# Thirteen of sixteen expert pairs through DRAM with a late read-back, and four smaller moves, in a fused two-block transformer kernel

## The chip, the cores and the metric

The kernel runs as one launch on one core of a Trainium2 chip. The metric is the device time of one execution in microseconds (us); the figure to compare is the median of several runs. The core's engines run side by side, each through its own instruction list in order: TensorE (PE in the profile, with its weight loads as PEld), VectorE (DVE), ScalarE (ACT), GpSimd (POOL) and SyncE (SP, which here only issues DMA transfers). They meet through semaphores. All of the core's transfers share 16 DMA engines.

## The reference

One input of 512 tokens by 1024 channels (float32) passes through two blocks. Cut to what matters here:

```
# first block
u  = rmsnorm(x) @ w_in
o1 = stick-breaking attention over u[:, :1536]     # 8 heads of 64, strictly causal:
     # z = q.k/8 ; weight[t,s] = sigmoid(z_ts) * prod_{s<j<t} sigmoid(-z_tj), s < t
o2 = rwkv7_group(u[:, 1536:])                      # gated delta-rule scan, 8 heads of 64
h  = x + concat(o1, o2) @ w_out
xn = rmsnorm(h)
# mixture of experts: best group of 4, best 2 of its 8 experts, weights c
for e in range(32):
    y += c[:, e] * ((silu(xn @ w_gate[e]) * (xn @ w_up[e])) @ w_down[e])   # 1024 -> 256 -> 1024
x  = rmsnorm(h + y) * final_norm_g
# second block: windowed and dilated attention, two gated branches, output projection, residual
```

Each expert has three weight matrices of 1 MB, so the 32 experts bring 96 MB from DRAM; each token uses two experts.

## The kernel before

Three phases follow each other.

**Phase 1** (`phase1`, to about 435 us) computes the first block up to `h`. A generator `mixing` emits the RWKV scan, and a generator `filler` emits the dense projections, the stick-breaking attention (`sb`) and the output projection; `mix` interleaves the two by credits, and a scheduler then sets each engine's final order. `sb(p)` treats two heads in 8 instances (query block `i`, head `h`). Stage `s0` makes scores on TensorE (`sbz`), two sigmoids on ScalarE (`sm` and `sp`), masks both on GpSimd (L804), takes the reversed running product of `sm` into a tile `I` on VectorE (L808, with one column of ones set by GpSimd, L807), and multiplies it into `sp` (L809). Stage `s1` transposes `sp` on TensorE into `sbw` (L817) and copies it to `wt` on ScalarE. Stage `s2` multiplies `wt` with the values (`sbo`, L829). In round j the loop emits `s0` of instance j, `s1` of j-1 and `s2` of j-2. The tiles `sm`, `sp`, `I` and `wt` share a ring of six buffers.

At the end of phase 1, `route(i)` normalises each block of 128 tokens and stores it into DRAM (`xr`, L1072, from ScalarE's queue). Expert weights are already being loaded then, through a ring of 18 buffers of 1 MB (`load`, `slot`; SP's queue).

**Phase 2** (`phase2`) chooses the experts, builds tables of token indices, and then goes through 16 pairs of experts q. GpSimd gathers the pair's rows of `xr` with an indirect DMA (64 slots for each expert; slots without a token move nothing). `ffn_up(q)` transposes them (`xgp`, `xgT`), multiplies with the gate and up weights (`gu`) and forms `hm`. `ffn_down(q)` transposes `hm` (`hT`, `hTs`) and multiplies with the down weights (`pd`). What follows depends on q:

- For q < EQ (8 before), the scaled output `y` is scattered by token into a DRAM array `yd` of 2 x 512 rows (first and second choice), zeroed early in phase 1.
- For the others, the output is split into two parts `yh`, `yl`; a one-hot matrix `C` (token by slot) is built on VectorE (L1297), and `combine` multiplies `C` with both parts on TensorE (`cb`, L1320: 16 matmuls per pair) and adds each product to the residual `hres` on VectorE (L1324).

`collect` reads `yd` back, one token block at a time from q = 9 on, into buffers of the same ring of 18 (`yt`, 1 MB each, on SP's queue between weight loads), and adds both choices to `hres` on VectorE. Emitted at q = 15, `ahead` loads the first weights of the second block (`w`, L1330) and `final_norm_g` (`fg`, L1338) and splits `w` into `wh`, `wl`. The last `ffn_down` is tied by `issue_after` to come behind that split in the order.

**Phase 3** is the second block. It begins by transposing `hres` (`x3T`, L1478), so it needs the finished sum.

Of the kernel before, what the change touches and what calls it, by code (L numbers as in the profile page):

```python
# [10 lines left out]
F = mybir.dt.float32  # L11
R = mybir.dt.float32r
# [3 lines left out]
OP = mybir.AluOpType  # L16
# [4 lines left out]
S, D = 512, 1024  # L21
NT = S // 128
# [4 lines left out]
CDEC = math.exp(-0.5)  # L27
EL = 6

EQ = 8  # L30

ER = 18
HB = 1
# [117 lines left out]
def rev(ap):  # L151
    n = ap.ap[-1][1]
    return bass.AP(tensor=ap.tensor, offset=ap.offset + (n - 1) * ap.ap[-1][0],
                   ap=[*ap.ap[:-1], [-ap.ap[-1][0], n]])
# [28 lines left out]
class K:  # L183
    def __init__(self, ctx, tc, a, dbg=None):
        self.ctx, self.tc, self.nc, self.a = ctx, tc, tc.nc, a
        self.dbg = dbg or {}
        self.C = {}

# [7 lines left out]
    def t(self, pool, name, shape, dt=F, tag=None, bufs=1):  # L196
        return pool.tile(shape, dt, name=name, tag=tag or name, bufs=bufs)
# [93 lines left out]
    def phase1(self):  # L291
        nc, a = self.nc, self.a
        tt, ts, stt = nc.vector.tensor_tensor, nc.vector.tensor_scalar, nc.vector.scalar_tensor_tensor
# [65 lines left out]
        r0, n = ROWS["shift_mu"]  # L359
        ts(self.omu, self.par[:, r0:r0 + n], -1.0, 1.0, op0=OP.mult, op1=OP.add)  # L360
        r0, n = ROWS["rw_k_a"]
# [5 lines left out]
        with self.tc.issue_after(par.ins):  # L367
            first = wsplit(None, (128, KD, 128), w0)
            for k in range(KD):
                x = xT[k // 4][:, k % 4, :]  # L370
# [414 lines left out]
        def sb(p):  # L785
            inst = [(i, h) for i in range(NT) for h in range(2)]
            st = {}
            s2_ = lambda name, shape=(128, 512): sb_(name, list(shape), tag="s2", bufs=6)

            def s0(i, h):  # L790
                N = 128 * (i + 1)
                if h == 0:

                    st["z"] = [self.p1("sbz", b) for b in ("pw", "pst")]
                    for z, r in zip(st["z"], (slice(0, 64), slice(64, 128))):
                        nc.tensor.matmul(z[:, 0:N], qk[p // 2][r, 2 * (p % 2), i * 128:(i + 1) * 128], qk[p // 2][r, 2 * (p % 2) + 1, 0:N], start=True, stop=True)
                pz = st["z"][h]
                sm = s2_("sm")
                nc.scalar.activation(sm[:, 0:N], pz[:, 0:N], AF.Sigmoid, scale=-0.125)
                sp = s2_("sp")  # L800
                nc.scalar.activation(sp[:, 0:N], pz[:, 0:N], AF.Sigmoid, scale=0.125)
                for z, fill in ((sm, 1.0), (sp, 0.0)):
                    d = z[:, N - 128:N]
                    nc.gpsimd.affine_select(out=d, in_=d, pattern=[[-1, 128]], base=0, channel_multiplier=1,  # L804
                                            compare_op=OP.is_gt, fill=fill)
                I = s2_("I", [128, 520])
                nc.gpsimd.memset(I[:, N:N + 1], 1.0)  # L807
                nc.vector.tensor_tensor_scan(rev(I[:, 0:N]), rev(sm[:, 0:N]), rev(sm[:, 0:N]), 1.0, op0=OP.mult, op1=OP.bypass)  # L808
                tt(sp[:, 0:N], sp[:, 0:N], I[:, 1:N + 1], op=OP.mult)  # L809
                st[i, h] = sp  # L810

            def s1(i, h):
                N = 128 * (i + 1)
                sp = st[i, h]
                pw = self.pb("sbw")
                for b in range(i + 1):
                    nc.tensor.transpose(pw[:, b * 128:(b + 1) * 128], sp[:, b * 128:(b + 1) * 128], eye)  # L817
                wt = s2_("wt")
                nc.scalar.activation(wt[:, 0:N], pw[:, 0:N], AF.Copy)
                st[i, h] = wt  # L820

            def s2(i, h):
                if (i, h) == (0, 0):
                    st["o"] = self.p1("sbo", "so")
                po, wt = st["o"], st.pop((i, h))
                o = slice((2 * i + h) * 64, (2 * i + h) * 64 + 64)
                c0 = (2 * p + h) * 64
                for b in range(i + 1):
                    nc.tensor.matmul(po[:, o], wt[:, b * 128:(b + 1) * 128], vs[:, b, c0:c0 + 64], start=(b == 0), stop=(b == i))  # L829

            def fin0():
                on = s2_("on")
                nc.scalar.activation(on, st["o"], AF.Copy)
                sq = s2_("sbsq")
                nc.scalar.activation(sq, on, AF.Square)
                q2 = sb_("sbs", [128, 8], bufs=2)
                nc.vector.tensor_reduce(q2, sq.rearrange("p (h t) -> p h t", t=64), axis=AX.X, op=OP.add)
                self.rsqrt(q2, q2, 1.0 / 64, 1e-6)
                ov = on.rearrange("p (h t) -> p h t", t=64)
                nc.gpsimd.tensor_tensor(ov, ov, q2[:, :, None].to_broadcast([128, 8, 64]), op=OP.mult)  # L840
                st["on"] = on

            def fin1():
                ps = self.pb("obT")
                for i in range(NT):
                    nc.tensor.transpose(ps[:, i * 128:(i + 1) * 128], st["on"][:, i * 128:(i + 1) * 128], eye)
                oT[p] = sb_(f"oT{p}", [128, 512])
                nc.scalar.activation(oT[p], ps, AF.Copy, scale=self.pc("sb_out_g", p))
                self.dump(f"osb{p}", oT[p])

            n = len(inst)
            for j in range(n + 2):
                if j == 2 and turn:
                    turn.pop()()
                if j < n:
                    s0(*inst[j])
                if 0 <= j - 1 < n:
                    s1(*inst[j - 1])
                if 0 <= j - 2 < n:
                    s2(*inst[j - 2])  # L860
                yield SU[0] * (inst[min(j, n - 1)][0] + 1)
            fin0()
            turn.append(fin1)
            yield SU[1]
# [191 lines left out]
    def route(self, i, xn, one):  # L1056

        nc, ss, rs = self.nc, self.rss, self.rrs
        x = xn
        nc.scalar.activation(x, self.h[:, i, :], AF.Square, accum_out=ss[:, i:i + 1])  # L1060
        self.rsqrt(rs[:, i:i + 1], ss[:, i:i + 1], 1.0 / D, 1e-6)
        yield
        xT = one("hT", [128, 8, 128], tag="wr", bufs=2)
        for c4 in range(2):
            ps = self.pb("hTp")
            for c in range(4):
                o = (4 * c4 + c) * 128
                nc.tensor.transpose(ps[:, c * 128:(c + 1) * 128], self.h[:, i, o:o + 128], self.ident)
            (nc.scalar.copy if c4 else nc.vector.tensor_copy)(xT[:, 4 * c4:4 * c4 + 4, :], ps.rearrange("p (c s) -> p c s", c=4))
        nc.scalar.activation(x.rearrange("p (c q) -> p c q", c=8), self.h[:, i, :].rearrange("p (q c) -> p c q", c=8),  # L1070
                             AF.Copy, scale=rs[:, i:i + 1])
        nc.scalar.dma_start(self.xr[i * 128:(i + 1) * 128, :], x)  # L1072
        yield
        for c in range(8):
            nc.tensor.matmul(self.pL[:, i * 36:(i + 1) * 36], xT[:, c, :], self.rw[:, c, :], start=(c == 0), stop=(c == 7))

    def phase2(self):
        nc, a = self.nc, self.a
        P2 = self.EB = self.tc.alloc_tile_pool(name="p2", bufs=1, reuse_waits="tile")
        P = P2  # L1080
        t = lambda name, shape, dt=F, **kw: self.t(P, name, shape, dt, **kw)
        tt, ts, red = nc.vector.tensor_tensor, nc.vector.tensor_scalar, nc.vector.tensor_reduce
        stt = nc.vector.scalar_tensor_tensor
        self.load(ER - self.nload)
        tb = self.t(self.E, "tb", [128, 16, 2])
        ti = self.t(self.E, "ti", [128, 16], I32)
        to = self.t(self.E, "to", [128, 16], I32)
# [155 lines left out]
        io = self.c("io512")  # L1243
# [22 lines left out]
            return hm  # L1266

        def ffn_down(q, hm):
            pT = self.pb("hT")
            for c in range(2):  # L1270
                nc.tensor.transpose(pT[:, c * 128:(c + 1) * 128], hm[:, c, :], self.ident)
            hT = t("hTs", [128, 2, 128], bufs=HB)
            nc.scalar.activation(hT, pT[:, 0:256].rearrange("p (c s) -> p c s", c=2), AF.Copy)  # L1273
            if q < EQ:
                y = t("y", [128, 1024], tag="y", bufs=4)
# [16 lines left out]
            if q < EQ:  # L1292
                nc.gpsimd.indirect_dma_start(out=self.yd[:], out_offset=bass.IndirectOffsetOnAxis(ap=to[:, q:q + 1], axis=0),
                                             in_=y, in_offset=None, bounds_check=2 * S - 1, oob_is_err=False)
                return None
            C = t("C", [128, 512], R, bufs=2)
            self.tc.keep_in_program_order(ts(C, io, tb[:, q, 0:1], None, op0=OP.is_equal))  # L1297
            return yh, yl, C

        def collect():  # L1300

            z = None
            for i in range(NT + 1):
                y = None
                if i < NT:
                    y = self.slot([128, 2, D], F, "yt")
                    nc.sync.dma_start(y, self.yd.rearrange("(j i p) f -> i p j f", j=2, p=128)[i])
                for j in range(2 if i else 0):
                    tt(self.h[:, i - 1, :], self.h[:, i - 1, :], z[:, j, :], op=OP.add)
                z = y  # L1310
                yield

        def combine(ys, last=False):
            for m in range(2 * NT):
# [47 lines left out]
        for q in range(17):  # L1362
# [6 lines left out]
            if q:  # L1369
                with ExitStack() as x:  # L1370
# [3 lines left out]
                    y = ffn_down(q - 1, up)  # L1374
                if y:
                    ys.append(y)
                self.load(6)
            if q > EQ:
                next(rows, None)
# [631 lines left out]
```

## Time and profile before

| what | value |
|---|---|
| median of 3 runs | 1320.55 us (1319.39 to 1325.21) |
| profiled execution | 1324.36 us, its span 1322.7 us |
| PE busy | 1227.2 us (93%) |
| DVE busy | 724.1 us (55%) |
| ACT busy | 485.0 us (37%) |
| POOL busy | 227.4 us (17%) |
| mean granted TensorE clock | 0.959 of full speed |
| DMA moved | 199.14 MB |

The span runs from the first to the last instruction; 1.66 us of the execution lie outside it. The shares are averages over three phases with different limits, so the stretches have to be read one by one. Times in the rows are from the span's start.

### The profile page before, as it was taken

How to read it: one execution, taken by the hardware profiler on the slowest of the kernel's cores; microseconds unless marked ns; L12 is line 12 of the kernel's file. 1: busy time of each engine (PE TensorE's matmuls, PEld its weight loads, DVE VectorE, ACT ScalarE, POOL GpSimd, SP SyncE). 2: the span in 40 equal slices, each digit the busy share in tenths (PEclk: the TensorE clock that was granted, in tenths of full speed). 3: DMA queues.
4: the chain of work that ended last, by engine and by line, in shares of the span. 5: the costliest groups of instructions: out<-in, count | busy, mean ns of one | idle time of the engine just before them, and what ended most of it. 6: DMA issues, size and time to landing. Idle time of an engine off the chain costs nothing.

```text
span 1322.7 us, 22028 instructions
## 1 busy us (share of the span) xinstructions
PE 1227.2 (93%) x8866; PEld 957.9 (72%) x8866; DVE 724.1 (55%) x1612; ACT 485.0 (37%) x994; POOL 227.4 (17%) x318
## 2 busy tenths in 40 slices
PE   6989998899889699988988999998999999999998
PEld 4778766667668455545545988887999887888888
DVE  5458666875656322223356656666545477633462
ACT  4433452553324201110013455556344573333231
POOL 2140143331420311100000422221132000000000
PEclk9969999988889699998989999999999999999999
DMA  8201111111238699999962521114211222422232
GB/s 313 77 32 50 64 49 33 33 64 49 72 137 341 256 384 424 421 422 423 424 255 80 192 81 59 62 65 99 97 65 65 97 67 65 159 90 70 80 137 72
DMA packets 45203, 199.14 MB, mean 151 GB/s; under 512 B 11659, under 2 KB 14129, under 8 KB 27944
## 3 DMA queue, kind: packets, MB, share of 16 engines
q1 hardware_dynamic: 31416, 176.09, 34.7%
q0 software_dynamic: 6640, 16.96, 3.9%
q10 hardware_dynamic: 7040, 4.61, 1.1%
q8 instruction: 72, 1.18, 0.4%
q14 instruction: 35, 0.29, 0.1%
HBM read 187.86 MB, written 16.27 MB: 154 GB/s over the span
## 4 chain that ended last, share of the span: by engine, by line
PE 52%; DVE 5%; ACT 4%; DMA 1%; issue 1%; POOL 1%; ACTq 0%; DVEq 0%; POOLq 0%
PE gu L1260 9%; PE tm L212 6%; PE tm L213 6%; PE tm L214 6%; PE pd L1283 4%; PE fm L213 4%; PE fm L214 4%; PE fm L212 4%; PE cb L1320 3%; ACT Pb L1652 2%; PE az L1641 1%; PE pbT L1858 1%; PE qT L1599 1%; DMA fd<-znt 1%; PE xgp L1251 1%
## 5 line engine op out<-in xcount | busy, mean ns | idle before, releaser
L212 PE MATMUL tm<-wh,ah 128*128 128x256 f32 x800 | 230.1, 288 | 5.9 <-ACT wh L203 5.2
L213 PE MATMUL tm<-wl,ah 128*128 128x256 f32 x800 | 226.1, 283 | 0.3 <-DVE wl L204 0.3
L214 PE MATMUL tm<-wh,al 128*128 128x256 f32 x800 | 226.2, 283 | 0.0
L203 ACT ACTIVATE wh<-w 128x1024 fp32r<-128x1024 f32 (+1 forms) x124 | 124.2, 1003 | 252.8 <-PE tm L213 96.2
L204 DVE TENSOR_TENSOR wl<-w,wh 128x1024 fp32r<-128x1024 f32 (+1 forms) x124 | 144.4, 1167 | 69.1 <-ACT wh L203 68.8
L212 PEld LDWEIGHTS tm<-wh,ah 128*128 128x128 f32 x800 | 151.5, 189 | 13.0 <-ACT wh L203 5.4
L214 PEld LDWEIGHTS tm<-wh,al 128*128 128x128 f32 x800 | 151.4, 189 | 1.7 <-issue 1.5
L213 PEld LDWEIGHTS tm<-wl,ah 128*128 128x128 f32 x800 | 151.8, 190 | 0.8 <-DVE wl L204 0.6
L1583 POOL TENSOR_TENSOR qss<-qss,nhalf 128x4 f32<-128x4 f32 x56 | 59.4, 1075 | 173.4 <-DVE qss L1582 173.4
L212 PE MATMUL u<-xh,wh 128*128 128x512 f32 x176 | 75.1, 427 | 5.0 <-ACT xh L371 4.1
L212 PE MATMUL fm<-ah,wh 128*128 128x512 f32 x192 | 76.1, 396 | 0.8 <-ACT vb L1766 0.8
L214 PE MATMUL fm<-ah,wl 128*128 128x512 f32 x192 | 76.1, 396 | 0.7 <-DVE wl L204 0.7
L213 PE MATMUL u<-xl,wh 128*128 128x512 f32 x176 | 74.3, 422 | 2.4 <-DVE xl L372 2.4
L213 PE MATMUL fm<-al,wh 128*128 128x512 f32 x192 | 75.9, 395 | 0.0
L214 PE MATMUL u<-xh,wl 128*128 128x512 f32 x176 | 73.2, 416 | 2.0 <-DVE wl L204 2.0
L1260 PE MATMUL gu<-eg,xgT 128*64 128x256 f32 x512 | 67.0, 397 | 2.4 <-DMA eg<-in_exp_w_gate_dram 2.0
L1283 PE MATMUL pd<-ed,hTs 128*64 128x512 f32 x256 | 64.8, 600 | 2.6 <-ACT hTs L1273 2.1
L1260 PE MATMUL gu<-eu,xgT 128*64 128x256 f32 x512 | 63.3, 380 | 0.0
L1264 DVE TENSOR_TENSOR hm<-hm,gu 128x256 f32<-128x256 f32 x16 | 6.7, 420 | 98.2 <-ACT hm L1263 98.2
L1263 ACT ACTIVATE hm<-gu 128x256 f32<-128x256 f32 x16 | 6.1, 383 | 145.7 <-PE gu L1260 101.2
L1260 PEld LDWEIGHTS gu<-eg,xgT 128*64 128x64 f32 x512 | 38.6, 142 | 26.4 <-issue 8.3
L1515 DVE TENSOR_TENSOR fm<-fm,rrb 128x512 f32<-128x512 f32 x24 | 26.0, 1083 | 57.2 <-PE fm L214 57.1
(418 smaller groups left out, 2490.3 us busy)
## 6 DMA issues: line engine op xcount, KB each, us to landing
w<-in_w_dram SPq DMA_DIRECT2D x33, 1024.0 KB, 4.9
eg<-in_exp_w_gate_dram SPq DMA_DIRECT2D x32, 1024.0 KB, 19.6
eu<-in_exp_w_up_dram SPq DMA_DIRECT2D x32, 1024.0 KB, 19.1
ed<-in_exp_w_down_dram SPq DMA_DIRECT2D x32, 1024.0 KB, 19.7
w<-in_wi_dram SPq DMA_DIRECT2D x22, 512.0 KB, 3.6
yd<-hres POOLq DMA_DIRECT2D x1, 4096.0 KB, 18.5
w<-in_wo_dram SPq DMA_DIRECT2D x8, 512.0 KB, 4.6
yt<-yd SPq DMA_DIRECT2D x4, 1024.0 KB, 19.8
```

The costliest lines, as they stand in the source:

```text
L203: i = nc.scalar.activation(hi, src, AF.Copy)
L204: j = nc.vector.tensor_tensor(lo, src, hi.bitcast(F), op=OP.subtract)
L212: mm(out, lh, rh, start=first, stop=False)
L213: mm(out, lh, rl, start=False, stop=False)
L214: mm(out, ll, rh, start=False, stop=last)
L1251: nc.tensor.transpose(ps[:, c * 128:(c + 1) * 128], xg[:, c2 * 4 + c, :], self.ident)
L1260: nc.tensor.matmul(ph[es, c0:c0 + 256], xt[:, c, es], EW[n, 2 * q + k][:, c, :], start=(c == 0), stop=(c == 7))
L1283: nc.tensor.matmul(pd[es, :], hT[:, c, es], EW["d", 2 * q + k][:, c, hf * 512:(hf + 1) * 512], start=(c == 0), stop=(c == 1))
L1320: nc.tensor.matmul(ps, C[:, i * 128:(i + 1) * 128], y[:, hf * 512:(hf + 1) * 512], start=(n == 0), stop=(n == 2 * len(ys) - 1))
L1515: tt(z, z, rrb.rearrange("p (l r) -> p r l", r=4), op=OP.mult)
L1583: nc.gpsimd.tensor_tensor(ss[:, i, :], ss[:, i, :], self.nhalf[:, 0:4], op=OP.pow)
L1652: nc.scalar.activation(Pt[:, n, j, 0:N], Pt[:, n, j, 0:N], AF.Exp, bias=nm[:, n, j:j + 1], scale=-1.0, accum_out=sm[:, n, j:j + 1])
```

## The change

Five things change; phase 3 is the same code.

1. EQ goes from 8 to 13, so pairs 8 to 12 scatter into `yd` too, and only pairs 13 to 15 go through `C` and `combine`.
2. `collect` issues all four reads of `yd` together, at q = 14. GpSimd sums the two choices of a block (128 x 1024), and VectorE adds the sum to `hres` (once instead of twice). `C` is now computed at the start of `ffn_down`.
3. In `sb`, the running product is written over `sm` and the tile `I` is gone; the ring of six holds three tiles an instance instead of four.
4. In round j the loop emits `s2` of j-3, `s1` of j-2 and then `s0` of j: each instance's transposes come a round later.
5. The fourth `xr` store goes through SP's queue, and the last weight loads of the first 18, all but one, come behind it.

```diff
-EQ = 8
+EQ = 13
...
-                sm = s2_("sm")
+                sm = s2_("sm", [128, 520])
...
-                I = s2_("I", [128, 520])
-                nc.gpsimd.memset(I[:, N:N + 1], 1.0)
-                nc.vector.tensor_tensor_scan(rev(I[:, 0:N]), rev(sm[:, 0:N]), rev(sm[:, 0:N]), 1.0, op0=OP.mult, op1=OP.bypass)
-                tt(sp[:, 0:N], sp[:, 0:N], I[:, 1:N + 1], op=OP.mult)
+                nc.gpsimd.memset(sm[:, N:N + 1], 1.0)
+                nc.vector.tensor_tensor_scan(rev(sm[:, 0:N]), rev(sm[:, 0:N]), rev(sm[:, 0:N]), 1.0, op0=OP.mult, op1=OP.bypass)
+                tt(sp[:, 0:N], sp[:, 0:N], sm[:, 1:N + 1], op=OP.mult)
...
-            for j in range(n + 2):
+            for j in range(n + 3):
...
+                if 0 <= j - 3 < n:
+                    s2(*inst[j - 3])
+                if 0 <= j - 2 < n:
+                    s1(*inst[j - 2])
                 if j < n:
                     s0(*inst[j])
-                if 0 <= j - 1 < n:
-                    s1(*inst[j - 1])
-                if 0 <= j - 2 < n:
-                    s2(*inst[j - 2])
...
-        nc.scalar.dma_start(self.xr[i * 128:(i + 1) * 128, :], x)
+        self.stored = (nc.sync if i == NT - 1 else nc.scalar).dma_start(self.xr[i * 128:(i + 1) * 128, :], x)
...
-        self.load(ER - self.nload)
+        self.load(1)
+        with self.tc.issue_after(self.stored.ins):
+            self.load(ER - self.nload)
...
         def ffn_down(q, hm):
+            if q >= EQ:
+                C = t("C", [128, 512], R, bufs=2)
+                self.tc.keep_in_program_order(ts(C, io, tb[:, q, 0:1], None, op0=OP.is_equal))
...
-            C = t("C", [128, 512], R, bufs=2)
-            self.tc.keep_in_program_order(ts(C, io, tb[:, q, 0:1], None, op0=OP.is_equal))
             return yh, yl, C
...
+            y = [self.slot([128, 2, D], F, "yt") for _ in range(NT)]
+            for i in range(NT):
+                nc.sync.dma_start(y[i], self.yd.rearrange("(j i p) f -> i p j f", j=2, p=128)[i])
+            yield
+            for i in range(NT):
+                nc.gpsimd.tensor_tensor(y[i][:, 0, :], y[i][:, 0, :], y[i][:, 1, :], op=OP.add)
+                tt(self.h[:, i, :], self.h[:, i, :], y[i][:, 0, :], op=OP.add)
+                if i % 2:
+                    yield
```

Three places of the resulting order follow; line numbers after `experts` are one lower or higher in the changed kernel.

SP's queue at the end of the weights, before; `eg`, `eu` and `ed` with the numbers from 5737 on are the gate, up and down weights of pair 15, and the three other `yt` reads stand in the same way ahead of pairs 12, 13 and 14:

```order
L1307 DMA yt<-yd 128x2x1024
L1053 DMA eg_5737<-in_exp_w_gate_dram 128x2048
L1053 DMA eg_5739<-in_exp_w_gate_dram 128x2048
L1053 DMA eu_5741<-in_exp_w_up_dram 128x2048
L1053 DMA eu_5743<-in_exp_w_up_dram 128x2048
L1053 DMA ed_5745<-in_exp_w_down_dram 128x2048
L1053 DMA ed_5747<-in_exp_w_down_dram 128x2048
L1330 DMA w_5824<-in_w_dram 128x2048
L1338 DMA fg<-in_final_norm_g_dram 128x1024
```

The same end of SP's queue, now:

```order
L1052 DMA eg_5585<-in_exp_w_gate_dram 128x2048
L1052 DMA eg_5587<-in_exp_w_gate_dram 128x2048
L1052 DMA eu_5589<-in_exp_w_up_dram 128x2048
L1052 DMA eu_5591<-in_exp_w_up_dram 128x2048
L1052 DMA ed_5593<-in_exp_w_down_dram 128x2048
L1052 DMA ed_5595<-in_exp_w_down_dram 128x2048
L1306 DMA yt<-yd 128x2x1024 x4
L1331 DMA w_5678<-in_w_dram 128x2048
L1339 DMA fg<-in_final_norm_g_dram 128x1024
```

The four reads stand between pair 15's last weights and the second block's first weights `w`.

VectorE at the end of phase 2, before, from pair 14's split to the last adds of `cb`:

```order
L207 SCALAR_TENSOR_TENSOR yl<-pd,tb,yh 128x512
L1297 TENSOR_SCALAR C<-cstio_3644,tb 128x512
L1264 TENSOR_TENSOR hm<-hm,gu 128x256
L1324 TENSOR_TENSOR hres<-hres,cb 128x512
L1265 TENSOR_TENSOR hm<-hm,gu 128x256
L1324 TENSOR_TENSOR hres<-hres,cb 128x512 x7
L204 TENSOR_TENSOR wl_5827<-w_5824,wh_5826 128x1024 x2
L207 SCALAR_TENSOR_TENSOR yl<-pd,tb,yh 128x512 x2
L1297 TENSOR_SCALAR C<-cstio_3644,tb 128x512
L1324 TENSOR_TENSOR hres<-hres,cb 128x512 x8
```

The same end of phase 2 on VectorE, now, from pair 14's `C` to the first of the eight last adds:

```order
L1272 TENSOR_SCALAR C<-cstio_3612,tb 128x512
L1310 TENSOR_TENSOR hres<-hres,yt 128x1024
L1325 TENSOR_TENSOR hres<-hres,cb 128x512 x2
L1310 TENSOR_TENSOR hres<-hres,yt 128x1024
L1325 TENSOR_TENSOR hres<-hres,cb 128x512 x4
L1310 TENSOR_TENSOR hres<-hres,yt 128x1024
L1325 TENSOR_TENSOR hres<-hres,cb 128x512 x2
L1310 TENSOR_TENSOR hres<-hres,yt 128x1024
L204 TENSOR_TENSOR wl_5681<-w_5678,wh_5680 128x1024 x2
L1272 TENSOR_SCALAR C<-cstio_3612,tb 128x512
L207 SCALAR_TENSOR_TENSOR yl<-pd,tb,yh 128x512
L1325 TENSOR_TENSOR hres<-hres,cb 128x512
```

All four adds of read-back sums stand in the last stretch, between the adds of `cb`, and ahead of the split of `w` and of pair 15's `C` and `yl`.

TensorE in the first rounds of `sb`, before; `u` is filler work, `oT`, `pg` and `bkT` are parts of the RWKV scan:

```order
L796 MATMUL sbz<-qk 128x256 x2
L212 MATMUL u<-xh,wh 128x512
L817 MATMUL sbw<-ident,sp 128x128
L730 MATMUL oT<-ident,O 64x64 x16
L736 MATMUL pg<-xgt,g_92 128x512
L829 MATMUL sbo<-vs,wt 128x64
L603 MATMUL bkT<-ident,bk 128x128 x4
L796 MATMUL sbz<-qk 128x384
```

The same place, now:

```order
L796 MATMUL sbz<-qk 128x256 x2
L212 MATMUL u<-xh,wh 128x512
L730 MATMUL oT<-ident,O 64x64 x16
L736 MATMUL pg<-xgt,g_92 128x512
L213 MATMUL u<-xl,wh 128x512
L603 MATMUL bkT<-ident,bk 128x128 x4
L214 MATMUL u<-xh,wl 128x512
L212 MATMUL u<-xh,wh 128x512
L213 MATMUL u<-xl,wh 128x512
L214 MATMUL u<-xh,wl 128x512
L816 MATMUL sbw<-ident,sp 128x128 x2
```

The transposes `sbw` stand behind more independent work.

## Rows read from the trace of the kernel before

**Rows 1.** Windows of phase 2 (length, busy by engine, granted clock, DMA share, GB/s):

```profile
540.00:611.00 71.00, 61.98 (x441) 35.17 (x439) 15.10 (x26) 7.19 (x14) 7.39 (x8) 1.00 1.01 422
611.00:680.00 69.00, 59.90 (x343) 34.84 (x340) 30.58 (x46) 7.27 (x14) 0.00 (x0) 0.90 1.00 419
680.00:722.00 42.00, 38.25 (x179) 21.08 (x176) 26.98 (x43) 9.03 (x15) 2.93 (x4) 0.96 0.22 83
```

**Rows 2.** SP's queue in order of time (start, length, issue):

```profile
594.52 0.39 SPq L1307 DMA_DIRECT2D yt<-yd  x1
...
647.62 0.38 SPq L1307 DMA_DIRECT2D yt<-yd  x1
...
664.82 0.33 SPq L1330 DMA_DIRECT2D w<-in_w_dram  x1
```

**Rows 3.** Tile `ed` from 640 to 720 us: last issues, time to landing:

```profile
L1053 SPq DMA_DIRECT2D ed<-in_exp_w_down_dram x4: 327/328/328, 642.8 to 662.4; - x4
...
DMA to landing us min/median/max: 19.6/19.6/19.6
```

**Rows 4.** DMA queues from 590 to 720 us (packets, MB, share):

```profile
q0 software_dynamic: 320, 0.49, 1.0%
```

**Rows 5.** Critical chain of two early pairs (start, length, what):

```profile
500.44 7.06 PE gu L1260 x64
...
512.86 7.06 PE gu L1260 x64
```

**Rows 6.** TensorE's groups from 682 to 722 us (busy, mean ns, idle before):

```profile
L1320 PE MATMUL cb<-yh,C 128*128 128x512 f32 x30 | 14.1, 470 | 2.8 <-DVE C L1297 2.1 <-DVE hres L1324 0.8
```

**Rows 7.** Timeline of phase 2's end (start, length, what, idle before):

```profile
702.93 1.90 POOL L1339 TENSOR_TENSOR fg<-fg 128x1024 f32<-128x1024 f32 x1 [95.91 <-PE gu L1260]
703.04 2.00 ACT L203 ACTIVATE wh<-w 128x1024 fp32r<-128x1024 f32 x2
...
708.87 3.65 PE L1283 MATMUL pd<-ed,hTs 128*64 128x512 f32 x16
...
709.58 2.35 DVE L204 TENSOR_TENSOR wl<-w,wh 128x1024 fp32r<-128x1024 f32 x2
...
713.96 0.48 DVE L1297 TENSOR_SCALAR C<-cstio,tb 128x512 fp32r<-128x512 f32 x1
714.58 0.47 PE L1320 MATMUL cb<-yh,C 128*128 128x512 f32 x1 [2.06 <-DVE C L1297]
...
716.34 0.63 PE L1320 MATMUL cb<-yh,C 128*128 128x512 f32 x1
...
719.14 1.89 DVE L1324 TENSOR_TENSOR hres<-hres,cb 128x512 f32<-128x512 f32 x3 [0.17 <-PE cb L1320]
```

**Rows 8.** GpSimd's groups over the span (busy, mean ns, idle before):

```profile
L510 POOL TENSOR_TENSOR kk<-al,kk 128x512 f32<-128x512 f32 x4 | 7.7, 1930 | 6.8 <-DVE rqv L507 6.8
...
L514 POOL TENSOR_TENSOR bk<-P,al 128x512 f32<-128x512 f32 x4 | 5.1, 1264 | 0.3
```

**Rows 9.** Tile `yt`: the adds on VectorE (ns min/median/max):

```profile
L1309 DVE TENSOR_TENSOR hres<-hres,yt x8: 1212/1217/1224, 616.6 to 687.5; 128x1024 f32<-128x1024 f32 x8
```

**Rows 10.** TensorE's waits from 140 to 430 us (total, times, longest):

```profile
PE sbw L817 <- DVE sp L809: 7.3, 7, 2.4
PE oT L730 <- POOL O L724: 5.9, 2, 4.0
```

**Rows 11.** Window of `sb`'s first half, columns as in rows 1:

```profile
215.00:285.00 70.00, 59.64 (x369) 43.97 (x366) 60.04 (x122) 31.01 (x66) 23.31 (x55) 0.90 0.14 48
```

**Rows 12.** Timeline after the router (start, length, what, idle before):

```profile
446.72 1.17 POOL L1230 DMA_INDIRECT xg<-xr,ti  x1 [0.90 <-DMA ed<-in_exp_w_down_dram]
...
450.84 0.39 PE L1217 MATMUL pJ<-metj,slotb 128*64 128x16 bf16 x8 [3.58 <-PEq L1392]
```

**Rows 13.** Issues of the whole span (KB each, us to landing):

```profile
hres<-x2d SPq DMA_DIRECT2D x1, 2048.0 KB, 10.8
```

**Rows 14.** Tile `sbw`: who waited for it (us, times):

```profile
  ACT wt L819: 43.8, 21
```

More of the change, by code (lines that the diff above doesn't have):

```diff
@@ L1295, in ffn_down @@
                 return None
-            C = t("C", [128, 512], R, bufs=2)
-            self.tc.keep_in_program_order(ts(C, io, tb[:, q, 0:1], None, op0=OP.is_equal))
             return yh, yl, C
         def collect():
[L1302 to L1311, printed above, removed]
+            y = [self.slot([128, 2, D], F, "yt") for _ in range(NT)]
[7 more added lines that the diff above has]
+                    yield
         def combine(ys, last=False):
```

## The prediction

> **What bounds the kernel now.** Reading goes from the page's shares to the stretches, since the shares mix three phases. Phase 2 comes first, by windows [rows 1]: from 540 to 611 us and from 611 to 680 the DMA engines are busy all the time (share 1.01 and 1.00) at 422 and 419 GB/s, while TensorE idles 9 us in each. So the stream of weights sets the pace there, not TensorE. After 680 us the DMA share is 0.22 and TensorE is busy 38.25 of 42 us: a backlog is worked off that the stream no longer explains. The reader should next see, in SP's queue, that four reads of `yd` stand among the last weights (first at 594.52, last at 647.62) [rows 2]. The last weight is issued at 662.4 and takes 19.6 us, so it lands at 682.0 [rows 3]. The sum `hres` is complete when the last adds of `cb` end: 719.14 + 1.89 = 721.03 us [rows 7]. That is 39.0 us after the last weight. Of the backlog, 30 pairs of `cb` matmuls lie behind 682 us (30 x 470 ns for the first of each, overlapping the second) [rows 6]. Phase 1 comes second, by waits: TensorE waits 7.3 us in all for `sp` before the transposes `sbw` [rows 10], in a stretch where VectorE is busy 60.04 of 70 us and TensorE's granted clock is 0.90 [rows 11].
>
> **The change, part by part.**
>
> *The stream.* Four reads of 1 MB leave the queue ahead of the last weights: 4 x 1.049 MB / 0.423 MB per us = 9.9 us earlier (0.42 being the rate of rows 1). Five more scatters enter. GpSimd's queue moved 0.49 MB in two gathers (and a few KB else) between 590 and 720 us [rows 4], so half-empty slots cost nothing, and a scatter of as many rows is 0.245 MB: 5 x 0.245 / 0.423 = 2.9 us. Net 7.0 us: the last weight lands at 675.0. TensorE must keep up with that. An early pair without `cb` takes 512.86 - 500.44 = 12.42 us [rows 5], and a pair's stream is (6.29 + 2 x 0.245) / 0.423 = 16 us, so it does, and its backlog is gone: pair 15's gate and up products end about 1 us before its last down weight lands.
>
> *The end of phase 2.* Behind the last weights now come four reads and `w`, each 1.049 / 0.423 = 2.48 us: the reads land at 677.5, 680.0, 682.4 and 684.9 us, and `w` at 687.4. Two chains follow, and both end at nearly the same time. First, `w` is behind the reads on SP, its split stands ahead of pair 15's `hTs` on ScalarE, as before, and `hTs` is what pair 15's `pd` waits for. The split takes 2.00 us (689.4), and with the copy behind it `pd` starts at about 689.9, where it started at 708.87 before; from there to the last add it was 721.03 - 708.87 = 12.2 us [rows 7], less 0.5 us for `C` no longer standing between the last `yl` and `cb`: 701.6. Second, GpSimd sums four blocks. The trace has no sum of two different 128 x 1024 tiles. One product of such a tile with itself took 1.90 us [rows 7], and 128 x 512 products of two tiles took 1.26 to 1.93, so twice that is 2.5 to 3.9 [rows 8]. I take 2.9, between, nearer the rows with two tiles: the sums end at 680.4, 683.3, 686.2 and 689.1. VectorE adds each (1.22) [rows 9] among eight adds of `cb`, all in one list, so a late sum holds the adds behind it and, through the two banks that `cb` alternates between, TensorE's `cb` matmuls, and `pd` behind these. By the list the fourth add ends at about 693; then the split of `w` (2.35), to 695.5, and from `C` to the end 721.03 - 713.96 = 7.1, plus one `yl` of 0.7 that now follows `C`: 703.3. TensorE has stood nearly idle since 675 and starts slow, as at 716.34 where one `cb` matmul takes 0.63 us [rows 7]; some 3.5 us at half speed cost 1.8 us on the first chain. So `hres` is complete at about 704 us: 17 us earlier. Ends: 702 us (no slow start, fast sums: a gain of 19), and 708 us (a gain of 13) or later if the reads run slowly, both below among the rivals. The 80 `cb` matmuls that go are 80 x 14.1 / 60 = 18.8 us [rows 6], of which the backlog was made; what is late next is `w`.
>
> *Less on VectorE and ScalarE in pairs 8 to 12* (no `C`, no `yl`) lies beside the stream and gives nothing more. The scatters' issues on GpSimd (a gather's took 1.17 [rows 12]) lie in its idle time, 63.6 of 71 us and more in these windows [rows 1].
>
> *`sb`.* The transposes `sbw` come a round later, behind other matmuls, and one buffer less a round is taken from the ring, so GpSimd's ones and VectorE's product wait for fewer releases. At most the 7.3 us of waits go, and with them part of the half-speed stretches (10% of 70 us at 0.90, so 7 us) [rows 10, 11]: 13 us at best. But VectorE is busy 86% of this stretch and its work is the same, so what TensorE saves it waits for elsewhere; and the new mixture can lengthen waits like the 5.9 us of `oT` for GpSimd [rows 10]: +6 at worst. I take -4, near half of the waits, since the waits are the row that the edit acts on.
>
> *The store of `xr`.* The gather waits 0.90 us for its last landing, but TensorE is held by its branch until 450.84 [rows 12]. That branch hides the gain, so 0. Without it the 0.9 us would show; three loads are issued later, for the third pair, which is two pairs of 12.42 us off [rows 5]. Ends -1 and +2.
>
> *Sum.* -17 - 4 + 0 = -21 us. Against the profiled execution of 1324.36 us that is 1303.4. The median of the runs shown, 1320.55, is 3.8 us below it; taken off that, the forecast is 1299.5 us.
>
> **The rivals.**
>
> *Sums and adds that exclude each other.* Rows of one form and size speak for it, which took 1.26 and 1.93 us on GpSimd [rows 8]; something else than their work slows the second. If no sum runs beside a VectorE add of two tiles, sums are 3.9 us and each of the last three also waits 1.22: the fourth ends at 677.5 + 4 x 3.9 + 3 x 1.22 = 696.8, its add at 698.0, the split of `w` at 700.4, the end at 708.2. The gain there is 13 and the time 1303.5. Against it: nothing in those rows names VectorE. The Trainium skill states such a rule (SBUF — State Buffer, Who interferes with whom): a VectorE instruction with two SBUF inputs and a GpSimd instruction that reads SBUF exclude each other, and the later one waits for all of the earlier. By that rule the second time holds; the trace has no two such instructions side by side that would show it here.
>
> *A slow read-back.* Alone on the queues, one 2 MB read took 10.8 us [rows 13], half the stream's rate. At 21.6 us for the four, `w` lands at about 699 and `hres` is complete near 716: 5 us of gain. Without a gain in `sb` that is 1315.5, with it 1311.5. Against it: six transfers are queued here, not one.
>
> *A gain at both upper ends*: 19 in phase 2 and 13 in `sb`, 1288.5.
>
> *Slower: `sb`'s rounds get longer.* With three tiles a round in a ring of six, `sp` of round j+2 takes the buffer of `sp` of round j, which is free only after that round's transposes, now two rounds late. ScalarE waits 43.8 us in 21 waits for `sbw` now, 2.1 each [rows 14]. If half of that, 1.05 us, were exposed in each of 32 rounds, phase 1 would take 34 us more, and the time is 1320.5 + 34 - 17 = 1337.5. It decides from 17 / 32 = 0.5 us a round. Against it: the copy `wt` that stands just ahead of that sigmoid on ScalarE waits for the same transposes already. For it: VectorE's load there leaves little slack.
>
> That the edits don't reach the bound can nearly be excluded: the reads do leave the stream, and 80 matmuls do leave the tail.
>
> **How the numbers follow.** Forecast (1293 to 1307) 58%; exclusive sums 14%; slow read-back 15%; both upper ends 6%; slower 7%. The range leaves out the slower case and parts of the last two beside it: 1289 to 1313 us. A measurement here tells 0.5%, 6.6 us, from no change, so faster means below 1313.9: 58 + 14 + 6 + a little under half of 15, or 84%; the rest of the read-back case, 9%, is no change; slower 7%.
>
> **What would show it.** Right: the last `ed` landing near 675 us, with the four `yt` landing in the 10 us behind it; pair 15's `pd` starting near 690, released by the split of `w`; `x3T` ending some 17 us earlier; waits of TensorE for `sp` before `sbw` below 3 us. Wrong: a DMA share below 1 before the last weight; `yt` landings spread over 20 us; sums of 4 us or more; GpSimd waiting for VectorE; in phase 1, ScalarE waiting longer for `sbw`, or TensorE leaving the branch later than 450.84. The prediction fails if phase 1 moves by more than 10 us either way, or if something other than `w` and the sums holds pair 15's `pd`.

## The result, and the profile after

The changed kernel takes 1306.97 us (median of 6 runs, 1304.37 to 1309.20); the kernel before took 1321.66 us in the runs beside it (median of 6). The ratio is 0.989, 95% interval 0.987 to 0.9911: faster by 14.7 us, where 21 were forecast. The median lies at the very end of the forecast's range (1293 to 1307). The profiled execution took 1309.20 us, its span 1307.5, so 15.2 us less than before's span. Where they lie, from the landmarks of both traces:

| landmark, us from the span's start | before | after | difference |
|---|---|---|---|
| TensorE leaves the branch into phase 2 | 450.84 | 449.43 | -1.4 |
| last expert weight landed | 682.0 | 676.8 | -5.2 |
| pair 15's `pd` starts | 708.87 | 693.34 | -15.5 |
| last add of `cb` ends | 721.03 | 705.61 | -15.4 |
| end of the span | 1322.7 | 1307.5 | -15.2 |

The 676.8 is worked out: the first read of `yd` has landed at 679.25, when GpSimd starts on it, and `w`, four transfers behind, at 689.05, which is 2.45 us for each; one of these ahead of 679.25. Phase 3 took the same time (601.7 and 601.9 us). So 1.4 us lie in phase 1 and 14.0 between the branch and the last add.

The windows of phase 2 again, with columns as in [rows 1]:

```profile
540.00:611.00 71.00, 59.39 (x424) 33.56 (x422) 13.47 (x23) 5.87 (x13) 10.13 (x10) 1.00 1.02 422
611.00:680.00 69.00, 55.14 (x376) 29.19 (x372) 13.38 (x24) 7.57 (x15) 2.72 (x3) 1.00 1.01 422
680.00:722.00 42.00, 32.58 (x192) 25.05 (x192) 35.40 (x55) 16.78 (x31) 16.76 (x10) 0.92 0.28 108
```

The stream still sets the pace to the last weight (share 1.01, 422 GB/s). TensorE is idle longer beside it (14 of 69 us, 9 before): the backlog is gone. SP's queue after (start, length, issue), against [rows 2, 3]:

```profile
654.25 2.76 SPq L1052 DMA_DIRECT2D ed<-in_exp_w_down_dram  x2
659.15 8.59 SPq L1306 DMA_DIRECT2D yt<-yd  x4
668.98 0.35 SPq L1331 DMA_DIRECT2D w<-in_w_dram  x1
```

The tail, rows of four engines' timelines (start, length, what, idle before), against [rows 7]:

```profile
677.77 0.39 PE L1321 MATMUL cb<-yl,C 128*128 128x512 f32 x1
...
679.25 11.46 POOL L1309 TENSOR_TENSOR yt<-yt 128x1024 f32<-128x1024 f32 x4 [42.22 <-DMA yt<-yd]
...
681.62 1.23 DVE L1310 TENSOR_TENSOR hres<-hres,yt 128x1024 f32<-128x1024 f32 x1 [4.77 <-POOL yt L1309]
...
682.95 1.28 DVE L1325 TENSOR_TENSOR hres<-hres,cb 128x512 f32<-128x512 f32 x2
...
683.69 0.79 PE L1321 MATMUL cb<-yh,C 128*128 128x512 f32 x1 [5.53 <-DVE hres L1325]
...
685.10 3.38 DVE L1310 TENSOR_TENSOR hres<-hres,yt 128x1024 f32<-128x1024 f32 x1 [0.87 <-POOL yt L1309]
...
688.58 1.28 DVE L1325 TENSOR_TENSOR hres<-hres,cb 128x512 f32<-128x512 f32 x2
...
689.05 2.01 ACT L203 ACTIVATE wh<-w 128x1024 fp32r<-128x1024 f32 x2 [13.51 <-DMA w<-in_w_dram]
...
690.97 0.36 ACT L1277 ACTIVATE hTs<-hT 128x256 f32<-128x256 f32 x1
...
693.34 3.65 PE L1287 MATMUL pd<-ed,hTs 128*64 128x512 f32 x16
...
694.93 1.23 DVE L1310 TENSOR_TENSOR hres<-hres,yt 128x1024 f32<-128x1024 f32 x1
...
696.07 2.35 DVE L204 TENSOR_TENSOR wl<-w,wh 128x1024 fp32r<-128x1024 f32 x2
...
701.34 4.27 DVE L1325 TENSOR_TENSOR hres<-hres,cb 128x512 f32<-128x512 f32 x7
```

The second add took 3.38 us where the first took 1.23 on the same shape. `pd` starts 2.0 us after `hTs` was there (691.33): the split of `w` did not hold it. What did, the critical chain shows (start, length, what):

```profile
681.73 3.35 POOL yt L1309
685.08 0.02 issue
685.10 3.39 DVE hres L1310
...
688.58 0.70 DVE hres L1325
689.28 0.04 issue
689.33 4.08 PE cb L1321 x16
693.40 1.89 PE pd L1287 x8
695.30 0.02 issue
695.32 0.70 ACT yh L206
696.02 0.06 issue
696.07 2.35 DVE wl L204 x2
698.43 0.40 DVE C L1272
```

A sum on GpSimd, then an add on VectorE, then pair 14's last `cb`, then `pd`. Behind `pd` VectorE's two instructions for the split of `w` come back into the chain, since they stand in its list ahead of pair 15's `C`. From 679.25 to 705.62 us VectorE is busy 21.25 of 26.4 us.

### The profile page after: what moved, and what is told of

It is laid out like the page before. It is cut to its first block, busy times and chain, and to the rows that moved or that the text cites. A ratio compares the mean times of both kernels' runs of the same rounds, so it can differ in the third digit from the quotient of the medians.

```text
span 1307.5 us, 21839 instructions
## 1 busy us (share of the span) xinstructions
PE 1202.3 (92%) x8786; PEld 939.3 (72%) x8786; DVE 699.4 (53%) x1574; ACT 481.0 (37%) x989; POOL 245.4 (19%) x327
## 4 chain that ended last, share of the span: by engine, by line
PE 43%; DMA 14%; DVE 4%; ACT 3%; POOL 1%; issue 1%; ACTq 0%; SPq 0%; DVEq 0%; POOLq 0%
PE tm L212 7%; PE tm L214 6%; PE tm L213 6%; DMA eu<-in_exp_w_up_dram 5%; DMA eg<-in_exp_w_gate_dram 5%; PE fm L214 4%; PE fm L213 4%; PE fm L212 4%; PE gu L1261 3%; DMA ed<-in_exp_w_down_dram 2%; PE az L1642 1%; PE pd L1287 1%; DMA yt<-yd 1%; PE pbT L1859 1%; PE qT L1600 1%
## 5 line engine op out<-in xcount | busy, mean ns | idle before, releaser
L1261 PE MATMUL gu<-eg,xgT 128*64 128x256 f32 x512 | 64.0, 385 | 1.0 <-DMA eg<-in_exp_w_gate_dram 0.6
L1287 PE MATMUL pd<-ed,hTs 128*64 128x512 f32 x256 | 61.2, 599 | 2.3 <-ACT hTs L1277 1.6
L1261 PEld LDWEIGHTS gu<-eu,xgT 128*64 128x64 f32 x512 | 38.3, 137 | 30.2 <-DMA eu<-in_exp_w_up_dram 12.2
```

The costliest lines, as they stand in the source:

```text
L1261: nc.tensor.matmul(ph[es, c0:c0 + 256], xt[:, c, es], EW[n, 2 * q + k][:, c, :], start=(c == 0), stop=(c == 7))
L1287: nc.tensor.matmul(pd[es, :], hT[:, c, es], EW["d", 2 * q + k][:, c, hf * 512:(hf + 1) * 512], start=(c == 0), stop=(c == 1))
```

## The experiments

All times below are medians; ratios are to the kernel before, run beside them. The runs were made in three groups, and the changed kernel itself was not run again in them, so a difference of 1 or 2 us between two of its variants is not told from none.

### `sb` alone, and `sb` undone

The edits 3 and 4 of the change alone in the kernel before:

```diff
-                I = s2_("I", [128, 520])
...
-                nc.vector.tensor_tensor_scan(rev(I[:, 0:N]), rev(sm[:, 0:N]), ...
+                nc.vector.tensor_tensor_scan(rev(sm[:, 0:N]), rev(sm[:, 0:N]), ...
...
-            for j in range(n + 2):
+            for j in range(n + 3):
...
```

> The kernel before with sb's two edits alone (running product written over sm, transposes a round later). Theory (sb gives some 3 us: in the profiles so far TensorE leaves the branch between 445.7 and 449.6 us with the edits and between 450.8 and 451.6 without): the branch ends between 445 and 450, and the time is 1317 to 1320. Rival (the single pair of profiles, 1.4 us, was jitter, and sb gives nothing): the branch ends above 450 and the time is 1322.

1319.49 us, ratio 0.9988 (0.9972 to 1.0003): 2.5 us by the medians, not told from none by its interval. The same lines taken back from the changed kernel:

> The changed kernel with sb's two edits undone (tile I, order of the rounds). Theory: sb gave what the changed kernel's branch shows, 450.84 - 449.43 = 1.4 us, so TensorE leaves the branch near 450.8 and the time is 1308.4 us (+1.4). Rival, as forecast: sb gave 4 us, the branch ends near 453.4 and the time is 1311. Second rival: sb gave nothing and the 1.4 us come from the store of xr: branch at 449.4, time 1307.

1308.97 us (0.9897, 0.9864 to 0.993), 2.0 us above the changed kernel by the medians and 0.9 by the ratios, which is not told from none either. The branch tells more than the times. With the two edits alone TensorE leaves it at 448.15, with them undone at 451.55 (timelines of TensorE, start, length, what, idle before):

```profile
448.15 0.39 PE L1216 MATMUL pJ<-metj,slotb 128*64 128x16 bf16 x8 [3.31 <-PEq L1391]
```

```profile
451.55 0.39 PE L1219 MATMUL pJ<-metj,slotb 128*64 128x16 bf16 x8 [3.70 <-PEq L1394]
```

Over all profiles of this study the branch ends between 445.74 and 449.62 us with the edits (11 profiles, mean 448.1) and at 450.84 and 451.55 without (2). So `sb` gives some 3 us by these means, an estimate, since only two profiles stand on the other side; one pair of profiles (-1.4) could not have told. The waits changed as said: TensorE's waits from 140 to 430 us in the run with `sb` alone (total, times, longest), against [rows 10]:

```profile
PE oT L730 <- POOL O L724: 5.3, 2, 3.5
PE sbw L816 <- DVE sp L808: 3.6, 4, 1.2
PE oT L730 <- POOL sm L806: 2.7, 1, 2.7
PE obT L845 <- POOL sm L806: 1.7, 1, 1.7
```

`sbw` waited 7.3 us for VectorE and 3.6 now. Some comes back: waits of `oT` and `obT` for the ones that GpSimd sets in `sm` are 4.4 us; for those in `I` they were 1.7.

### The fourth store undone

```diff
-        self.stored = (nc.sync if i == NT - 1 else nc.scalar).dma_start(...)
+        nc.scalar.dma_start(...)
...
-        self.load(1)
-        with self.tc.issue_after(self.stored.ins):
-            self.load(ER - self.nload)
+        self.load(ER - self.nload)
```

> The changed kernel with the fourth store of xr back on ScalarE's queue and the loads of the first 18 not held behind it. Theory: the branch hides this edit: TensorE leaves it at 449.4, time 1307 (0 to +1). Rival: the three held loads cost the stream some 1.3 MB behind 440 us, so without the edit the last weight lands up to 3 us earlier and the time is 1304.

1307.61 us (0.9896, 0.9868 to 0.9924): no difference from the changed kernel. The branch ends at 448.17, inside the spread above. The rival falls: from the branch to the first landed read of `yd` it is 230.7 us here and 229.8 in the changed kernel, so the three loads held behind the store cost the stream nothing that can be told.

### The late read-back without the five pairs

```diff
-EQ = 13
+EQ = 8
...
-            if q > EQ:
+            if q > 13:
                 next(rows, None)
```

> The changed kernel with EQ back at 8 (pairs 8 to 12 go through the one-hot matmuls) and the read-back still late. It tells the late read-back from the five more pairs. Theory (the five pairs' 80 cb matmuls are the backlog behind the last weight, and the reads alone only turn waiting for weights into a longer backlog): the last weight lands some 10 us earlier than before, hres is complete 4 to 8 us earlier than before, 1312 to 1317. Rival (the late read-back gives the whole gain, the five pairs nothing): 1306 to 1308.

1313.64 us (0.9943, 0.9922 to 0.9965), as the theory had it: of the 14.7 us, the five pairs give 6.7 (with the read-back late), and the rest of the change 8, some 2 to 3 of it `sb`. This run also prices the scatters. SP's queue (start, length, issue):

```profile
652.77 8.65 SPq L1306 DMA_DIRECT2D yt<-yd  x4
```

Its GpSimd starts on the first landed read at 672.88, 223.3 us after its branch (449.62). In eight profiles with EQ 13 the first read has landed 227.6 to 230.7 us after the branch, median 228.8. So five scatters cost the stream 5.6 us, 1.1 each; against the lowest and the highest of the eight it is 4.4 and 7.4. Moved bytes of GpSimd's queue, from the pages of before and after:

```profile
q0 software_dynamic: 6640, 16.96, 3.9%
```

```profile
q0 software_dynamic: 7360, 18.49, 4.4%
```

1.53 MB for five is 0.306 MB each, 0.72 us at 0.423 MB per us. They differ by pair: in the changed kernel the same queue moved 0.36 MB from 620 to 636 us, where pair 11's scatter ran alone, and 0.27 MB from 636 to 660 us, in pair 12's. The other 0.4 us of each are not explained by bytes; with one profile at EQ 8 that stays open.

### Do sums and adds exclude each other?

VectorE's four adds are held until GpSimd's last sum is done: the add of the last block comes first.

```diff
                 nc.gpsimd.tensor_tensor(y[i][:, 0, :], y[i][:, 0, :], y[i][:, 1, :], op=OP.add)
-                tt(self.h[:, i, :], self.h[:, i, :], y[i][:, 0, :], op=OP.add)
...
+            for i in (3, 2, 1, 0):
+                self.tc.keep_in_program_order(tt(self.h[:, i, :], self.h[:, i, :], y[i][:, 0, :], op=OP.add))
```

> The changed kernel with VectorE's four read-back adds held until GpSimd's last sum is done (the add of the last block comes first), so that no sum runs beside an add. Theory (a sum and an add of two SBUF tiles exclude each other): each of the four sums takes 2.34 us, as the one that stood alone did, and each add 1.23; the sums end by 2.45 us landings at 8 us after the first one starts and a sum, some 9.7 us in all instead of 11.46. Rival (a sum of 128x1024 takes 2.3 to 3.4 us by itself): 11.5 us again, sums of 3.3 us among them. The time of the whole: 1305 to 1309.

Tile `yt` in the changed kernel (ns min/median/max), then in this run:

```profile
L1309 POOL TENSOR_TENSOR yt<-yt x4: 2337/2865/3357, 679.2 to 687.4; 128x1024 f32<-128x1024 f32 x4
L1310 DVE TENSOR_TENSOR hres<-hres,yt x4: 1226/1319/3377, 681.6 to 694.9; 128x1024 f32<-128x1024 f32 x4
```

```profile
L1309 POOL TENSOR_TENSOR yt<-yt x4: 2337/2372/2403, 673.5 to 681.0; 128x1024 f32<-128x1024 f32 x4
```

```profile
673.48 9.81 POOL L1309 TENSOR_TENSOR yt<-yt 128x1024 f32<-128x1024 f32 x4 [41.56 <-DMA yt<-yd]
...
693.62 4.62 DVE L1312 TENSOR_TENSOR hres<-hres,yt 128x1024 f32<-128x1024 f32 x4
```

Four sums in 9.81 us instead of 11.46, none above 2.40. They do exclude each other: a sum is 2.34 to 2.40 us alone and 3.36 with an add ahead of it, and an add waits out a sum that began before it (3.38). Adds of `cb`, whose second input is in PSUM, ran beside the sums at 0.69 us each, as ever. The Trainium skill states this rule (SBUF — State Buffer, Who interferes with whom): a VectorE instruction with two SBUF inputs and a GpSimd instruction that reads SBUF keep each other out. These traces agree with it. The run itself took 1308.6 us (0.9904, 0.9872 to 0.9936): the adds stand later in the list, and from the first landing to phase 3's first matmul it takes 31.0 us, against 26.4 in the changed kernel.

Then the sums themselves were taken from GpSimd:

```diff
-                nc.gpsimd.tensor_tensor(y[i][:, 0, :], y[i][:, 0, :], y[i][:, 1, :], op=OP.add)
-                tt(self.h[:, i, :], self.h[:, i, :], y[i][:, 0, :], op=OP.add)
+                for j in range(2):
+                    tt(self.h[:, i, :], self.h[:, i, :], y[i][:, j, :], op=OP.add)
```

> The changed kernel with GpSimd's sums taken away: VectorE adds both choices itself (8 adds of 1.22 us). Theory (a sum on GpSimd and a VectorE add of two SBUF tiles exclude each other: one add took 3.38 us): all eight adds take 1.22, the last ends at about 693 to 695 instead of 696.1, and the sum over the whole kernel is 1 to 3 us faster, 1304 to 1306. Rival (VectorE's load sets the end, 4 x 1.22 more): 1310 to 1312.

1305.52 us (0.9885, 0.9854 to 0.9917), not told from the changed kernel. The time lies in the theory's range, but not for its reason: the last of the eight adds ends 19.4 us after the first landing, and the last of the four in the changed kernel 16.9. From the first landing to phase 3's first matmul it takes 27.7 us, against 26.4: VectorE is then busy 24.64 us. So GpSimd's sums are worth about 1 us by this pair of profiles and nothing by the medians, not the 4.9 us of four adds.

### Is it the split of `w`?

Pair 15's down stage is no longer tied behind the split:

```diff
-                    if q == 16:
+                    if q == 99:
                         for i in self.pin:
                             x.enter_context(self.tc.issue_after(i))
```

> The changed kernel without the tie of pair 15's down stage behind the split of w. Theory (the list of VectorE with the read-back's adds sets the end, not the split of w): pd of pair 15 runs from about 678 instead of 693.3, but the fourth read-back add still ends near 696 and the split of w near 698, so 8 adds of cb end near 703.6: 2 us faster, 1305. Rival (the split of w ahead of hTs sets the end, as the forecast had it): the end comes 6 us or more earlier, 1300.

1307.16 us (0.989, 0.9863 to 0.9918): nothing, where the theory had 2 us and the rival 6. `pd` ran 16 us earlier, and TensorE then waited for VectorE (TensorE's timeline):

```profile
677.35 3.65 PE L1287 MATMUL pd<-ed,hTs 128*64 128x512 f32 x16
...
682.92 0.50 PE L1321 MATMUL cb<-yh,C 128*128 128x512 f32 x1 [1.91 <-DVE hres L1325]
...
688.54 0.69 PE L1321 MATMUL cb<-yh,C 128*128 128x512 f32 x1 [3.51 <-DVE hres L1325]
...
701.32 0.47 PE L1321 MATMUL cb<-yh,C 128*128 128x512 f32 x1 [3.23 <-DVE hres L1325]
```

VectorE's list, with the read-back in it, sets the end: from the first landing to phase 3's first matmul it takes 28.0 us, against 26.4 with the tie. The wait of `hTs` for `w` does not set it. The 2.35 us in which VectorE splits `w` are part of that list all the same: here they run from 698.22, straight behind the last add of the read-back, and the eight last adds of `cb` stand behind them.

### Attempts at a better tail

Pairs 14 and 15 are summed in one last round of `cb` (8 adds fewer), and the tie is gone:

```diff
-            if len(ys) == 2 or q == 16:
+            if ys and q < 16:
                 combine(ys)
...
```

> The changed kernel, with pair 13 summed by itself, pairs 14 and 15 together in one last round of cb (8 adds on VectorE fewer behind the last weight), and no tie of pair 15's down stage to the split of w. Theory (what VectorE has in its list between the first landing of the read-back and the end sets the end: 8 adds of 0.64 us go, and pd runs before the read-back lands): the first tm comes 6 to 9 us earlier from the first landing than 26.4 us, 1298 to 1301. Rival (GpSimd's sums and the split of w set the end by themselves: 11.5 us of sums, then an add and the split of w, 3.6): 1303 to 1305.

1306.3 us (0.9882, 0.9856 to 0.9908), no gain, and neither the theory nor the rival. All engines' timeline shows the new wait:

```profile
685.45 2.58 POOL L1340 TENSOR_TENSOR fg<-fg 128x1024 f32<-128x1024 f32 x1 [1.39 <-DMA fg<-in_final_norm_g_dram]
...
686.20 2.11 DVE L1272 TENSOR_SCALAR C<-cstio,tb 128x512 fp32r<-128x512 f32 x1
...
688.46 0.77 PE L1321 MATMUL cb<-yh,C 128*128 128x512 f32 x1 [6.30 <-DVE C L1272]
```

`C`, 0.48 us in the changed kernel, waited for GpSimd's product of `fg`, and `cb` for `C`. So the next run computes pair 15's `C` earlier, squares `fg` on ScalarE, and puts ScalarE's first squares of `hres` behind the split of `w`:

```diff
+            if EQ <= q < 16:
+                CS[q] = t("C", [128, 512], R, bufs=2)
...
-            nc.gpsimd.tensor_tensor(self.fg2, self.fg, self.fg, op=OP.mult)
+            nc.scalar.activation(self.fg2, self.fg, AF.Square)
...
```

> The changed kernel with pairs 14 and 15 joined and no tie of pair 15's down stage (as in the run of that name), and besides: pair 15's C computed ahead of the read-back, the square of fg on ScalarE instead of GpSimd, the first squares of the second block behind the split of w on ScalarE. Theory (in the joined run C waited for GpSimd's product of fg, 2.11 us instead of 0.48, and cb for C, 6.3 us): that idle time goes, hres is complete some 22 us after the first landing of the read-back (26.4 in the changed kernel), and the time is 1301 to 1304. Rival (what is gained ahead of phase 3 is lost in its first 10 us, where VectorE has the squares and the splits to do): 1305 to 1307.

1310.04 us (0.9909, 0.9877 to 0.994): neither the theory nor the rival. The first `tm`, phase 3's first matmul, comes 25.6 us after the first landing, not 22: `cb` still waits for VectorE between its two banks. And phase 3 starts slower. Windows from the first `tm` on, columns as in [rows 1], in this run and in the changed kernel:

```profile
704.59:712.40 7.81, 6.53 (x27) 5.95 (x28) 7.81 (x16) 5.58 (x10) 0.00 (x0) 0.50 0.00 0
```

```profile
705.62:715.62 10.00, 9.49 (x76) 8.89 (x77) 9.95 (x21) 8.49 (x15) 0.00 (x0) 1.00 0.01 2
```

TensorE's granted clock is 0.50 in the first 7.8 us of phase 3, the lower of its two levels (1.2 GHz), and 1.00 in the changed kernel. Before that TensorE had run `cb` in short pieces, with waits of 2.42, 0.95 and 0.35 us for VectorE between them. From the first `tm` to the end it then takes 606.4 us, against 601.9. The run with the pairs joined shows the same, smaller: its first `tm` comes 25.5 us after the landing, the granted clock is 0.50 for the next 6.0 us, and the rest takes 604.5 us. So the 0.8 and 0.9 us that these two runs gain ahead of phase 3 are more than lost behind it. How much of that is the clock (at half speed 7.8 us cost at most 3.9), and how much VectorE, which is busy all the time in both windows, no run separates. With the sums on VectorE as well:

> As the reordered tail, with the sums on VectorE (eight adds of 1.22 us, nothing on GpSimd). Theory (a sum on GpSimd is worth it only while VectorE is short of time, and there it blocks VectorE's adds): within 2 us of the reordered tail, 1302 to 1306. Rival (VectorE's 4.9 us more are on the path): 4 to 5 us slower than the reordered tail.

1306.65 us (0.989, 0.986 to 0.992), just above the theory's 1302 to 1306, and 3.4 us below the reordered tail where the rival had 4 to 5 us above it; the granted clock is 1.00 in phase 3's first 10 us. And the joined pairs with EQ 14, whose generator is advanced once too few, so that the read-back of two of the four blocks is left out:

> As the run with pairs 14 and 15 joined, and pair 13 goes through DRAM too (EQ 14). Theory (pair 13's cb lies beside the stream, its scatter costs the stream 0.7 us): the same time within 2 us, 1298 to 1302. Rival (the reads of yd have to wait for pair 13's scatter and come late): 3 us or more slower than the run with EQ 13.

1304.33 us (0.9865, 0.9836 to 0.9893) with that work left out; it says nothing on EQ 14. No version beats the changed kernel by more than these measurements tell.

## Why the prediction was right, and where its sizes were off

- **The bound.** Right. The stream paces phase 2, and the five pairs' `cb` was the backlog: with the read-back late and EQ at 8 the kernel stays 6.7 us behind.
- **The stream: -7.0 forecast.** From the branch to the last weight it took 231.2 us before and 220.8 with late reads alone: -10.4 where -9.9 was worked out. The scatters were mis-sized: 5.6 us instead of 2.9, partly since they moved 0.306 MB each and not 0.245. The forecast took the two gathers of [rows 4], which are those of pairs 14 and 15, for pairs 8 to 12, which hold more rows. Some 2.7 us of the miss.
- **The read-back's rate.** Right: 2.45 us a read, full speed. The rival of a slow read-back, taken from the lone read of [rows 13], falls.
- **`w` gates pair 15's `pd`.** Wrong as to what ends last. `hTs` was ready at 691.33 (689.9 forecast, 1.4 late with the stream), but `pd` stood behind `cb`, and `cb` behind VectorE. The forecast names this path in its second chain, and still lets the split release `pd`. The run without the tie shows it: `pd` 16 us earlier, no gain.
- **Sums of 2.9 us.** The mean came out at 2.87, by chance: 2.34 for the work and 1.02 of waiting in two of four. The rival of sums and adds that exclude each other had the mechanism, which the forecast put at 14%, with too high a price for the sum (3.9); GpSimd waiting for VectorE stood among the signs of being wrong, and it came. What the forecast left out is the other side: an add waiting 2.15 us for a sum, with pair 14's adds and `cb` behind it. The fourth add ended at 696.2 instead of 693: 1.8 us from the late landing, the other 1.4 from this.
- **From the fourth add to the end.** 10.3 us forecast, 9.4 measured. From the last weight to the last add it is then 28.8 us where 29.0 were forecast: the late fourth add and the shorter end nearly cancel, and that the total came out is luck.
- **`sb`: -4.** Nearly right, as far as can be told: about -3 over all profiles, -2.5 and -2.0 us by the two pairs of medians, neither told from none. The waits at `sbw` fell to 3.6 us, not below 3.
- **The store: 0.** Right.

So the sum of -21 was too large by about 3 us in the end of phase 2 (-14.0 from branch to last add, -17 forecast), all of it ahead of the last weight (-3.8 from the branch to there, where -7.0 was forecast), and, in the profiled pair, by 2.6 in phase 1; the medians agree with the pair (-14.7). The cause that the forecast gave, less stream and less backlog, holds, and the median fell just inside its range; of the tail, the total was right and the path through it was not.

## What to carry to other kernels

When work is moved from VectorE to GpSimd to relieve VectorE, read from the trace which of their instructions read two SBUF tiles side by side: a 2.34 us sum saved a 1.22 us add and then held another for 2.15. Where several chains end within 3 us of each other, as `w` and the sums did here, taking one away gained nothing. Look past the end of the stretch too: two versions of the tail lost more behind the start of phase 3, whose first 6 to 8 us ran at the lower granted clock, than the 1 us that they had gained ahead of it. And a term of 1 or 2 us far ahead in the program can't be read from one pair of profiles: compare a wait, or the same landmark over several.

## What the runs showed that was not expected

- A VectorE instruction with one SBUF input was held by GpSimd too: `C` took 2.11 us beside a product on GpSimd, 0.48 alone. The Trainium skill (SBUF — State Buffer, Who interferes with whom) says that this operation can be held so in its modes that use both ports; the trace agrees that it is held, and does not show the mode. In the run with the adds behind the sums the split of `w`, which has two SBUF inputs, took 4.06 us instead of 2.35 beside the product of `fg`.
- The same phase 1 (but for the store of `xr` in two of them), to the branch, ended between 445.74 and 449.62 us in 11 profiles.
- A scatter of 0.306 MB into DRAM cost the stream 1.1 us, more than its bytes at the stream's rate (0.72), by one profile at EQ 8 against eight at EQ 13.
